# Decoder layer on one core: stores of keys issued by ScalarE, last pass in other parts, other ranks and buffers

## The chip, the core and the metric

The kernel runs on one core of a Trainium2 chip. Such a core has a tensor engine for matmuls (PE, with its weight loads shown as PEld), a vector engine (DVE), a scalar engine (ACT), GpSimd (POOL) and a sync engine (SP). Each takes its instructions strictly in the order of its own program; semaphores order them against each other. Transfers between DRAM and the on-chip memory (SBUF) are issued by an engine's queue and carried out by sixteen DMA engines. Matmuls write to PSUM, a small memory of eight banks, from which DVE or ACT copies.

The metric is the device time of one execution in microseconds; a kernel is run several times and the median is given. A profiled execution leaves a trace with every instruction, its start, its duration and what it waited for.

## The reference, cut to what matters

One inference step of a decoder layer: 512 new prompt tokens and 8 sample tokens of running sequences, model width 1024, float32. One projection of the input feeds two mixers, a gated linear attention (4 heads) and a dilated window attention (8 heads of 64); each result is multiplied by a SiLU gate, both go through one output projection, and a residual with LayerNorm closes the layer. The new keys and values are outputs too.

```python
SPLITS = (H_A * DK_A, H_A * DK_A, D_A, GATE_RANK, D_A, D_B, D_B, D_B, D_B)   # qa ka va za ga qb kb vb gb
...
for window, dil in DILATED_GROUPS:              # (128,1), (512,4), (2048,16)
    dist = jnp.arange(window // dil + 1) * dil
    idx = q_idx[:, None] - dist[None, :]        # row < 0 masked
    logits = einsum('bqhd,bqjhd->bhqj', q, k[idx]) * scale + rel_bias[t5_bucket(dist)]
    m = max(logits); p = exp(logits - m); s = sum(p)
    outs.append(einsum('bhqj,bqjhd->bqhd', p, v[idx]) / s)
...                                             # merged, weighted by their denominators
x = LayerNorm(alpha * x + concat(o_a * silu(g_a), o_b * silu(g_b)) @ w_out)
outputs: y_prompt, y_sample, state_gla_prompt, state_gla_sample, k_win_prompt, v_win_prompt, k_win_sample_new, ...
```

## The kernel before

**Arithmetic.** A float32 product is made of three matmuls in a faster format: a value is split into a high and a low part (`hi`, `lo`), and hi*hi, lo*hi and hi*lo are added in PSUM. ACT makes the high part of a weight, DVE the low part. PE runs one long list of such products, stage after stage (`ORDER`: qa, qb, kb, vb, gb and so on, the letters for query, key, value and gate of mixer a or b and a number for the column tile); this is the generator `dense`. Between the dense products stand the small matmuls of the mixers.

**Who sets the order.** No engine's order is written by hand. A planner in the kernel (`Plan`) takes tasks, which are generators that yield instructions, and at build time it takes in each step the instruction that could start first by its own table of costs (`Op.__init__`); among equals the lower rank goes first, the second argument of `add(task, rank)`. Instructions of PE that are not dense must be ready `SPARE` (800 ns) before their place. A transfer is costed with the time of its issue (`c`, another for SP than for the other issuer), a transfer time, and `LATE` when the DMA engines are thought to be busy. Buffers come from pools (`SLOTS`: `st` for strips, `t1` for small tiles, `w` for weights and so on), PSUM banks from three (`BANKS`: `d` for dense products, `s` for scores and weighted values, `t` for turns and other small ones). A task waits until its buffer is free. So a changed cost, rank or number of buffers moves instructions on all engines. Everything that is planned is recorded at line 377, and therefore tiles and not lines name things in the profile. In the listings below a number behind a name only tells one buffer from the next.

**The names that matter here.**
- `kw`: the new keys, turned into rows, in two tiles. `keys_store(i)` writes each to DRAM in eight stores of 64 KB, each as 512 runs of 128 bytes. `D` is SP's queue, `S` ACT and its queue, `V` DVE, `T` PE.
- `strip`: a strip of the table of position biases (`tabr`), 128 KB, one for two halves of a head's scores; DVE adds it to the scores (`pr<-ps_s,strip`) and takes their maximum, ACT makes the exponential (`pr`), PE turns the result (`ps_pt`), DVE or ACT copies it (`pt`), and PE multiplies with the values (`ps_pv`).
- `ps_turn`: values that are turned from columns to rows on PE, copied to `v`. `ps_sl`: scores of the sample tokens. Both take a `t` bank.
- `past`, `qbc`, `vv`, `pb`: the sample tokens' old keys, queries, old values and weights; POOL multiplies them, DVE reduces (`lt`, `o_pv`).
- `gb_s`: the sample tokens' gated result of mixer b. ACT and DVE split it (`mhb`, `mlb`); the first matmuls of the output projection (`ps_yf`) read both parts. `ps_oat`: the turned result of mixer a.
- `last_norm`: the last 128 rows of the output. DVE scales and shifts them in three parts, each stored as soon as it is ready. Four small operations on one column (`half`, `root`, in the profile `tail`) stand ahead.

## Time and profile before

| | us |
|---|---|
| median of three runs (276.99, 277.11, 278.33) | 277.11 |
| profiled execution | 277.73 |
| its span, from the first to the last instruction | 275.3 |
| PE busy | 266.1 |
| DVE busy | 214.0 |
| ACT busy | 157.5 |
| POOL busy | 54.3 |

The tensor engine's granted clock is 0.994 of full speed over the span. In the rows that follow, a time is followed by a duration; `out<-in` names what an instruction writes and reads; in square brackets stands the idle time of the engine just before, and what ended it. `SPq` and `ACTq` are the issues of transfers on SP and ACT; how long one takes is not how long the transfer takes. The table of stretches gives the busy time of each engine in a window of the span.

### The profile page before, as it was taken

How to read it: one execution, taken by the hardware profiler on the slowest of the kernel's cores; microseconds unless marked ns; L12 is line 12 of the kernel's file. 1: busy time of each engine (PE TensorE's matmuls, PEld its weight loads, DVE VectorE, ACT ScalarE, POOL GpSimd, SP SyncE). 2: the span in 40 equal slices, each digit the busy share in tenths (PEclk: the TensorE clock that was granted, in tenths of full speed). 3: DMA queues.
4: the chain of work that ended last, by engine and by line, in shares of the span. 5: the costliest groups of instructions: out<-in, count | busy, mean ns of one | idle time of the engine just before them, and what ended most of it. 6: DMA issues, size and time to landing. Idle time of an engine off the chain costs nothing.

```text
span 275.3 us, 7455 instructions
## 1 busy us (share of the span) xinstructions
PE 266.1 (97%) x2881; PEld 250.8 (91%) x2881; DVE 214.0 (78%) x582; ACT 157.5 (57%) x474; POOL 54.3 (20%) x71
## 2 busy tenths in 40 slices
PE   8999999999999999998999999999999999999990
PEld 5999999999999999987989989999999999998890
DVE  4835999998999587877696973737979999239984
ACT  4817966465637574957686824535668886224401
POOL 3000000000355080804000544745431000000000
PEclk9999999999999999999999999999999999999997
DMA  7977784436967798775497959896895660980432
GB/s 210 348 184 185 213 254 132 124 101 173 294 193 161 179 312 218 254 118 140 116 258 192 228 173 225 230 271 172 248 260 147 194 208 12 299 226 0 186 123 76
DMA packets 61527, 52.58 MB, mean 191 GB/s; under 512 B 13645, under 2 KB 53715, under 8 KB 61493
## 3 DMA queue, kind: packets, MB, share of 16 engines
q1 hardware_dynamic: 61061, 51.79, 67.6%
q8 instruction: 22, 0.36, 0.5%
q10 hardware_dynamic: 432, 0.33, 0.4%
q14 instruction: 12, 0.10, 0.1%
HBM read 46.02 MB, written 6.42 MB: 190 GB/s over the span
## 4 chain that ended last, share of the span: by engine, by line
PE 75%; DMA 9%; DVE 6%; SPq 4%; ACT 2%; issue 1%; POOL 1%; DVEq 0%; ACTq 0%
PE ps_ga L377 9%; PE ps_yf L377 9%; PE ps_qb L377 8%; PE ps_y L377 7%; PE ps_gb L377 6%; DMA strip<-tabr 6%; PE ps_qa L377 4%; PE ps_ka L377 4%; PE ps_va_f L377 4%; PE ps_va L377 4%; SPq L377 4%; PE ps_vb L377 3%; DMA qbc<-qsd 2%; PE ps_vb_f L377 2%; PE ps_pv L377 2%; ACT pr L377 2%
## 5 line engine op out<-in xcount | busy, mean ns | idle before, releaser
L377 POOL TENSOR_TENSOR past<-past,qbc 128x256 f32<-128x256 f32 x32 | 24.6, 803 | 101.1 <-DMA qbc<-qsd 92.4
L377 POOL TENSOR_TENSOR vv<-vv,pb 128x256 f32<-128x256 f32 x32 | 27.3, 887 | 51.9 <-DVE far L377 25.0
L377 ACT ACTIVATE pr<-pr,ms 128x128 f32<-128x128 f32 (+3 forms) x48 | 22.7, 489 | 9.7 <-DVE ms L377 9.6
L377 DVE CUSTOM_DVE_ANT_0 pr<-ps_s,strip 128x128 f32<-128x128 f32 (+3 forms) x32 | 11.7, 408 | 7.9 <-PE ps_s L377 4.4
L377 ACT COPY pt<-ps_pt 128x256 f32<-128x256 f32 (+1 forms) x26 | 8.9, 358 | 9.2 <-PE ps_pt L377 9.2
L377 ACT ACTIVATE sg<-sg 128x264 f32<-128x264 f32 (+1 forms) x32 | 13.4, 420 | 0.5
L377 PE MATMUL ps_ka<-xx,hi_ka 128*128 128x264 f32 (+1 forms) x64 | 12.5, 291 | 0.0
L377 PE MATMUL ps_pt<-cf,pr 128*128 128x128 f32 x56 | 10.8, 276 | 1.2 <-DVE v L377 1.2
L377 DVE TENSOR_REDUCE lt<-past 128x8 f32<-128x512 f32 x16 | 10.7, 673 | 1.1 <-POOL past L377 1.0
L377 PEld LDWEIGHTS ps_ka<-xx,hi_ka 128*128 128x128 f32 x64 | 10.1, 195 | 0.3 <-ACT hi_ka L377 0.3
L377 ACT ACTIVATE d<-d 128x512 f32<-128x512 f32 x11 | 6.9, 646 | 5.6 <-DVE d L377 5.6
L377 DVE TENSOR_REDUCE o_pv<-vv 128x4 f32<-128x1024 f32 x8 | 9.7, 1213 | 0.0
L377 ACT COPY feat_y<-ps_yf 128x256 f32<-128x256 f32 x7 | 2.6, 373 | 11.2 <-PE ps_yf L377 11.2
L377 PE MATMUL ps_ka<-xx,lo_ka 128*128 128x264 f32 (+1 forms) x32 | 8.7, 283 | 0.0
L377 PEld LDWEIGHTS ps_pt<-cf,pr 128*128 128x128 f32 x56 | 6.8, 140 | 1.7 <-DVE v L377 1.4
L377 DVE SCALAR_TENSOR_TENSOR y<-y,ps_yt 128x256 f32<-128x256 f32 x8 | 3.0, 418 | 6.9 <-PE ps_yt L377 6.9
L377 DVE SCALAR_TENSOR_TENSOR s<-v,ka_s,s 128x128 f32<-128x128 f32 x16 | 5.1, 343 | 3.2 <-DMA v<-vad 2.1
L377 PE MATMUL ps_qa<-xx,hi_ka 128*128 128x264 f32 (+1 forms) x32 | 7.2, 304 | 0.0
L377 PE MATMUL ps_s<-kp,qh 64*128 64x256 f32 (+1 forms) x64 | 7.0, 304 | 0.1
L377 PE MATMUL ps_pv<-pt,v 128*64 128x128 f32 (+1 forms) x80 | 6.9, 318 | 0.0
L377 DVE TENSOR_TENSOR d<-b 128x1024 f32<-128x1024 f32 (+1 forms) x6 | 6.8, 1129 | 0.0
L377 PE MATMUL ps_gb<-xx,hi_gb__1903 128*128 128x264 f32 (+1 forms) x32 | 6.8, 295 | 0.0
(570 smaller groups left out, 1060.7 us busy)
## 6 DMA issues: line engine op xcount, KB each, us to landing
past<-in_ck_dram SPq DMA_DIRECT2D x8, 512.0 KB
vv<-in_cv_dram SPq DMA_DIRECT2D x8, 512.0 KB
pb<-psd_s SPq DMA_DIRECT2D x16, 256.0 KB
s<-in_state_dram SPq DMA_DIRECT2D x4, 512.0 KB
strip<-tabr SPq DMA_DIRECT2D x16, 128.0 KB
qbc<-qsd SPq DMA_DIRECT2D x8, 256.0 KB
y<-in_xp_dram SPq DMA_DIRECT2D x4, 512.0 KB
x_raw<-in_xT_dram SPq DMA_DIRECT2D x6, 260.0 KB
```

What stands on the lines that cost most here:

```text
L377: getattr(eng.eng, op.fn)(*op.args, **op.kw)
```

## The change

The sixteen stores of `keys_store` are issued by ACT in place of SP. The last pass of `last_norm` goes in parts of 256, 512 and 256 columns in place of 512, 256, 256, with stores by ACT, SP and ACT in place of SP, ACT and SP, and the small operation `half` stands ahead of the wide one. One strip buffer fewer, one small tile more; four banks for scores and one for turns in place of three and two. In the planner's costs a transfer of an engine other than SP now takes 450 ns to issue, and a late one is 600 ns later. `va0` comes ahead of three `gb` tiles in the dense order. Sixteen ranks are new.

```diff
-    t2=2, st=3,
+    t2=2, st=2,
...
-    t1=5, ob=3,
+    t1=6, ob=3,
...
-BANKS = dict(d=3, s=3, t=2)
+BANKS = dict(d=3, s=4, t=1)
...
-LATE = 1000.0
+LATE = 1600.0
...
-ORDER = "qa0 qb0 qb1 qb2 qb3 kb0 kb1 vb0 kb2 kb3 gb0 vb1 gb1 gb2 va0 gb3 va1 ga0 ga1 ga2 ga3".split()
+ORDER = "qa0 qb0 qb1 qb2 qb3 kb0 kb1 vb0 kb2 kb3 gb0 vb1 va0 gb1 gb2 gb3 va1 ga0 ga1 ga2 ga3".split()
...
-            c = 640 if eng.name == "SP" else 100
+            c = 640 if eng.name == "SP" else 450
...
-                yield D.dma_start(kw_p[:, c:c + 32].rearrange("(b i) j -> i b j", i=32), kw[a * 32:a * 32 + 32, m])
+                yield S.dma_start(kw_p[:, c:c + 32].rearrange("(b i) j -> i b j", i=32), kw[a * 32:a * 32 + 32, m])
...
-        yield V.scalar_tensor_tensor(y[:, x], ps, mean, B["gamma"][:, x], op0=ALU.subtract, op1=ALU.mult)
         yield S.activation(root, ss, AF.Ln, scale=1.0 / DM, bias=q)
         yield V.tensor_scalar(half, ss, -0.5 / DM, dev, op0=ALU.mult, op1=ALU.add)
+        yield V.scalar_tensor_tensor(y[:, x], ps, mean, B["gamma"][:, x], op0=ALU.subtract, op1=ALU.mult)
...
-        for i, c in enumerate((slice(2 * GW, DM), slice(GW, 2 * GW), x)):
+        for i, c in enumerate((slice(3 * GW, DM), slice(GW, 3 * GW), x)):
             yield V.scalar_tensor_tensor(y[:, c], y[:, c], half, B["beta"][:, c], op0=ALU.mult, op1=ALU.add)
-            yield (S if i == 1 else D).dma_start(y_p[t * P:t * P + P, c], y[:, c])
+            yield (D if i == 1 else S).dma_start(y_p[t * P:t * P + P, c], y[:, c])
...
-    add(mix_sample_b(), 12.3)
+    add(mix_sample_b(), 18.3)
```

The other new ranks, before and after: `weight_splits` 50.7, 47.7; `gate_decay` 19.3, 1.7; `seed_sum` 13.2, 12.2; `bias_table` 25.3, 31.3; `sample_values` 14.3, 22.3; `sample_v` of `vnt` 21.3, 13.2 and of `vat` 21.3, 1.7; `sample_past` 22.3, 3.3; `sample_state` 61, 60; `values_store` 17.7, 17.3; `mix_tiles` 12.7, 11.7.

**The stores of keys.** SP's queue before, where the first tile of keys is stored; ahead of the stores stand the loads of a strip and of the sample's queries and keys, behind them strips:

```order
L377 DMA strip_1330<-tabr 128x1x256
L377 DMA strip_1330<-tabr 128x1x64
L377 DMA qbc_1305<-qsd 128x512
L377 DMA past_1380<-in_ck_dram 128x1024
L377 DMA out_dram<-kw_1133 32x16x32 x5
L377 DMA raw_vb__1415<-in_w_in_dram 128x4x256
L377 DMA out_dram<-kw_1133 32x16x32 x3
L377 DMA strip_1467<-tabr 128x1x256
L377 DMA strip_1467<-tabr 128x1x64
L377 DMA strip_1502<-tabr 128x1x256
```

ACT now, at the same tile:

```order
L377 ACTIVATE kp_1233<-ps_kb_1_1290 128x256
L377 COPY pt_1285<-ps_pt_1334 128x256
L377 DMA out_dram<-kw_1137 32x16x32 x2
L377 COPY pt_1285<-ps_pt_1378 128x128
L377 DMA out_dram<-kw_1137 32x16x32
L377 COPY vnt<-ps_vb_f_1345 128x8
L377 COPY feat<-ps_vb_f_1345 128x256
L377 DMA out_dram<-kw_1137 32x16x32
L377 ACTIVATE kd<-kd 128x1024
L377 ACTIVATE pr_1319,ms_1363<-pr_1319,ms_1363 128x128
L377 ACTIVATE pr_1319,ms_1364<-pr_1319,ms_1364 128x256
L377 ACTIVATE el<-b 128x16
```

Five and three stores in a row on SP are now two, one, one, one and three on ACT, between copies out of PSUM and exponentials; SP keeps its other rows.

**The strip of head 7 and the t bank.** The strip that DVE reads for head 7's first half, on SP: before (strip_2102; strip_1906 is head 5's) and now (strip_2218; strip_2031 is head 5's):

```order
L377 DMA out_dram<-kw_1717 32x16x32
L377 DMA qbc_1947<-qsd 128x512
L377 DMA strip_2102<-tabr 128x1x256
L377 DMA strip_2118<-tabr 128x1x256
L377 DMA strip_2118<-tabr 128x1x64
L377 DMA raw_va__2163<-in_w_in_dram 128x4x256
L377 DMA strip_2195<-tabr 128x1x256
```

```order
L377 DMA strip_2010<-tabr 128x1x256
L377 DMA strip_2031<-tabr 128x1x256
L377 DMA cts_raw<-in_c_t_dram 66x258
L377 DMA raw_gb__2154<-in_w_in_dram 128x8x128
L377 DMA strip_2196<-tabr 128x1x256
L377 DMA strip_2218<-tabr 128x1x256
L377 DMA raw_va__2272<-in_w_in_dram 128x4x256
L377 DMA strip_2287<-tabr 128x1x256
```

DVE now, from the second read of strip_2031 to the reads of strip_2218 (ISA is the addition with its maximum):

```order
L377 ISA pr_2159,ms_2178<-ps_s_2161,strip_2031 128x256
L377 ISA ms_2178 128x1
L377 RECIPROCAL ms_2177<-ms_2177 128x1
L377 TENSOR_SCALAR pr_2159<-pr_2159,ms_2177 128x128
L377 COPY v_1978<-ps_vb_3_2148 128x256
L377 RECIPROCAL ms_2178<-ms_2178 128x1
L377 TENSOR_SCALAR pr_2159<-pr_2159,ms_2178 128x256
L377 COPY pt_2052<-ps_pt_2209 128x256
L377 TENSOR_TENSOR lo_gb__2227<-raw_gb__1714,hi_gb__2226 128x1024
L377 ISA pr_2246,ms_2264<-ps_s_2248,strip_2218 128x128
L377 ISA ms_2264 128x1
L377 ISA pr_2246,ms_2265<-ps_s_2248,strip_2218 128x256
```

ACT now, in the same place; pr_2246 is what DVE makes with strip_2218:

```order
L377 ACTIVATE pr_2159,ms_2178<-pr_2159,ms_2178 128x256
L377 CAST hi_gb__2226<-raw_gb__1714 128x1024
L377 CAST hi_gb__2269<-raw_gb__1892 128x1024
L377 ACTIVATE pr_2246,ms_2264<-pr_2246,ms_2264 128x128
L377 ACTIVATE pr_2246,ms_2265<-pr_2246,ms_2265 128x256
L377 COPY v_1978<-ps_turn 128x2x128
L377 ACTIVATE pr_2245,ms_2262<-pr_2245,ms_2262 128x128
```

PE now; ps_turn is the bank that the COPY above reads, and ps_sl is the next in a `t` bank:

```order
L377 MATMUL ps_turn<-cf,feat 128x128 x2
L377 MATMUL ps_pv_2268<-far_1795,vp_1574 64x256
L377 MATMUL ps_pv_2268<-far_1833,vp_1574 64x256
L377 MATMUL ps_pv_2268<-far_2053,vp_1574 64x256
L377 MATMUL ps_pv_2268<-far_2084,vp_1574 64x256
...
L377 MATMUL ps_pv_2268<-pt_1794,v_1344 64x256 x2
L377 MATMUL ps_pv_2268<-pt_2052,v_1344 64x256 x2
L377 MATMUL ps_pv_2268<-pt_1794,v_1344 64x128 x2
L377 MATMUL ps_pv_2268<-pt_2052,v_1344 64x128 x2
L377 MATMUL ps_sl<-cts,rb 66x258
L377 MATMUL ps_va_f_2224<-xx_300,hi_va__1931 128x264
```

With two strip buffers, strip_2218 is loaded when strip_2031 has been read; with three, strip_2102 was loaded when the strip of head 4 had been read. The copy of ps_turn, which was DVE's, is ACT's and stands behind two exponentials of pr_2246, and PE's ps_sl waits for the bank.

**The split of gb_s.** DVE before, from the sum that completes gb_s to its low part, mlb:

```order
L377 TENSOR_TENSOR vnt<-vnt,o_pv 128x32
L377 TENSOR_REDUCE wsum<-raw_wo__3372 128x2
L377 TENSOR_TENSOR gb_s<-gb_s,vnt 128x32
L377 TENSOR_TENSOR newton<-rmss 128x4
L377 TENSOR_SCALAR ssq<-ssq 128x4
L377 CAST hi_wo__3586<-wsum 128x2x2
L377 TENSOR_TENSOR newton<-newton,ssq 128x4
L377 TENSOR_SCALAR ssq<-rmss 128x4
L377 TENSOR_TENSOR lo_wo__3587<-wsum,hi_wo__3586 128x2x2
L377 TENSOR_TENSOR mlb_2020<-gb_s,mhb_2019 128x2x8
L377 SCALAR_TENSOR_TENSOR rmss<-newton,ssq 128x4
L377 TENSOR_SCALAR oa_3156<-ps_oa_3510,rmss 128x128
```

DVE now:

```order
L377 TENSOR_TENSOR vnt<-vnt,o_pv 128x32
L377 TENSOR_REDUCE wsum<-raw_wo__3335 128x2
L377 TENSOR_TENSOR ga_3070<-ps_ga_0_3610,sg 128x256
L377 TENSOR_TENSOR ga_s<-ps_ga_0_3610,sg 128x8
L377 TENSOR_TENSOR gb_s<-gb_s,vnt 128x32
L377 CAST hi_wo__3625<-wsum 128x2x2
L377 SCALAR_TENSOR_TENSOR ga_s<-o_as,gn,ga_s 128x8x4
L377 SCALAR_TENSOR_TENSOR ga_3070<-ps_oat,gn,ga_3070 128x2x128
L377 TENSOR_TENSOR mlb_1982<-gb_s,mhb_1981 128x2x8
L377 TENSOR_TENSOR mla_3680<-ga_s,mha_3679 128x4x8
L377 SCALAR_TENSOR_TENSOR ga_3070<-ps_oat,gn,ga_3070 128x2x64
L377 TENSOR_TENSOR mlb_2764<-gb_s,mhb_2763 128x2x8
```

A gate (ga from ps_ga) now stands ahead of gb_s, and the first read of ps_oat ahead of mlb; the split stood in front of both.

22 lines of the change are left out of this document (11 added, 11 removed).

## The prediction

> **What bounds the kernel now.** I read the page first, then the table of stretches, the waits of the tensor engine, and the timeline at the one place where it waits. The page's busy line and its two hardware DMA queues (packets, MB, share of sixteen engines):
>
> ```profile
> PE 266.1 (97%) x2881; PEld 250.8 (91%) x2881; DVE 214.0 (78%) x582; ACT 157.5 (57%) x474; POOL 54.3 (20%) x71
> q1 hardware_dynamic: 61061, 51.79, 67.6%
> q10 hardware_dynamic: 432, 0.33, 0.4%
> ```
>
> PE is busy for 266.1 of 275.3 us, and the program of matmuls does not change, so what can be gained is a share of the 9.2 us in which PE stands. The waits of PE, and the stretches (stretch, its length, busy time of PE, PEld, DVE, ACT, POOL, granted clock, DMA share, GB/s):
>
> ```profile
> PE warm_ps L377 <- DVE warm L1844: 1.2, 1, 1.2
> PE ps_pt L377 <- DVE v L377: 1.2, 1, 1.2
> ```
> ```profile
> 125.00:150.00 25.00, 23.82 (x271) 21.76 (x266) 18.31 (x68) 17.02 (x54) 2.93 (x4) 1.00 0.64 176
> ...
> 250.00:275.00 25.00, 18.70 (x107) 16.01 (x106) 20.31 (x54) 6.74 (x27) 0.00 (x0) 0.94 0.29 106
> ```
> ```profile
> 75.00:95.00 20.00, 19.87 (x175) 19.30 (x174) 16.93 (x38) 12.15 (x34) 8.43 (x10) 1.00 0.70 174
> ```
>
> One wait stands at the start, which the change leaves; one lies in 125 to 150 us. Of the rest, 6.3 us are the tail after the last matmul, in the stretch from 250. This is a kernel bound by PE with one repairable hole. The hole in the timelines, PE and then DVE (start, duration, instruction, idle time before and its releaser):
>
> ```profile
> 127.58 0.28 PE L377 MATMUL ps_vb<-hi_vb__1584,xx 128*128 128x256 f32 x1
> 129.04 0.44 PE L377 MATMUL ps_pt<-cf,pr 128*128 128x128 f32 x2 [1.18 <-DVE v L377]
> ```
> ```profile
> 126.82 0.29 DVE L377 CUSTOM_DVE_ANT_0 pr<-ps_s,strip 128x128 f32<-128x128 f32 x1 [1.29 <-DMA strip<-tabr]
> 128.58 0.41 DVE L377 COPY v<-ps_turn 128x256 f32<-128x256 f32 x1
> ```
>
> DVE stood 1.29 us for a strip of the bias table; the copy of ps_turn stood behind that in DVE's order, and PE needed the bank that this copy frees. The strip was late behind the stores of keys: SP issued them in these pieces (with the strips just ahead), and the tile's row gives the least, median and greatest time of one; the last row is a store that ACT issued:
>
> ```profile
> 70.58 5.40 SPq L377 DMA_DIRECT2D strip<-tabr  x4
> ...
> 78.62 6.92 SPq L377 DMA_DIRECT2D out_dram<-kw  x5
> ...
> 86.14 2.47 SPq L377 DMA_DIRECT2D out_dram<-kw  x3
> ...
> 114.72 4.99 SPq L377 DMA_DIRECT2D out_dram<-kw  x6
> ```
> ```profile
> L377 SPq DMA_DIRECT2D out_dram<-kw x16: 315/530/1936, 78.6 to 120.2; - x16
> ```
> ```profile
> 271.79 0.36 ACTq L377 DMA_DIRECT2D out_dram<-y  x1
> ```
>
> **The change, part by part.** The sum is made against the profiled execution, 277.73 us (275.3 of span and 2.4 around it); that stands 0.6 above the runs' median of 277.11, which I take off at the end. 0.5% is 1.4 us, about what a measurement of this kernel can tell from no change.
>
> *The old stall, -1.2.* In the new order no PE instruction waits at that place on a DVE copy behind this strip's read: the dense stage of vb is over before the read. I count the 1.18 us as gone (between 0 and -1.3).
>
> *Two strips in place of three, +1.0.* Each strip load now waits for the read of the strip two before. The tight one is strip_2218. SP issues it after DVE's second read of strip_2031; ACT's copy of ps_turn stands behind the two exponentials of the scores that DVE reads with strip_2218; and ps_sl needs the bank of that ps_turn, since only one t bank is left. So a strip's flight again ends in a wait of PE. Its length is a race between two times from the last ps_s matmul of heads 4 and 5. The rows for it, from the chain, from DVE and from PE:
>
> ```profile
> 65.31 6.56 DMA strip<-tabr
> ...
> 121.19 5.49 DMA strip<-tabr
> ...
> 127.15 0.99 ACT pr L377 x4
> ...
> 129.63 1.42 PE ps_vb L377 x12
> ```
> ```profile
> 118.98 0.67 DVE L377 TENSOR_REDUCE lt<-past 128x8 f32<-128x512 f32 x1
> ...
> 119.94 0.24 DVE L377 CUSTOM_DVE_ANT_0 pr<-ps_s,strip 128x128 f32<-128x128 f32 x1
> ...
> 121.09 0.39 DVE L377 CUSTOM_DVE_ANT_0 pr<-ps_s,strip 128x256 f32<-128x256 f32 x1
> ...
> 122.97 0.36 DVE L377 TENSOR_SCALAR pr<-pr,ms 128x256 f32<-128x256 f32 x1
> ```
> ```profile
> 120.99 0.44 PE L377 MATMUL ps_s<-kp,qh 64*128 64x128 f32 x4
> ...
> 122.19 1.52 PE L377 MATMUL ps_pv<-far,vp 128*64 128x256 f32 x16
> ...
> 125.38 0.44 PE L377 MATMUL ps_turn<-cf,feat 128*128 128x128 f32 x2
> 125.65 0.27 PE L377 MATMUL ps_pt<-cf,pr 128*128 128x128 f32 x1
> ```
>
> The strip's side: the matmul's own 0.28; four reads of strips, which ran from 119.94 to 121.48, 1.5, with a reduction of lt (0.67), a scaling (0.36) and a copy (0.41) now among them: 3.0; flight 5.49; 0.14 until DVE starts (126.68 to 126.82); two reads to the end of the second, 0.6; its exponential, half of the four in 0.99, 0.5; the copy, 0.4. Sum 10.4; the nine instructions that DVE has between those reads are hidden in the flight. PE's side, up to ps_sl: 38 dense matmuls at 0.12 (twelve in 1.42), 4.5; six turns at 0.14 (two from 125.38 to 125.65), 0.8; twelve scores, 0.9 of the 1.2 from 120.99 to 122.19, which hold three dense ones too; the weighted values, 125.38 - 122.19 = 3.2. Sum 9.4. PE waits for 1.0. With a flight of 6.56 it is 2.1; with one under 4.5 it is 0. I take 5.49, the row of the same strip before, and keep 0 to 2.1.
>
> *ps_yf, +0.3.* The sample's gated attention output is now split at the last moment. Its rows before:
>
> ```profile
> 213.53 1.22 DVE L377 TENSOR_REDUCE o_pv<-vv 128x4 f32<-128x1024 f32 x1
> ...
> 217.31 0.17 DVE L377 TENSOR_TENSOR mlb<-gb_s,mhb 128x16 fp32r<-128x16 f32 x1
> ...
> 219.25 1.91 DVE L377 SCALAR_TENSOR_TENSOR ga<-ps_oat,gn,ga 128x256 f32<-128x256 f32 x6
> ```
> ```profile
> 217.92 1.03 PE L377 MATMUL ps_oat<-cf,oa 128*128 128x128 f32 x8
> ...
> 219.74 0.28 PE L377 MATMUL ps_yf<-mlb,hi_wo__3233 128*128 128x264 f32 x1
> ```
>
> Before, mlb was there at 217.48 for a matmul at 219.74, 2.3 us early. Now a read of ps_oat stands ahead of it on DVE. From the last ps_oat matmul DVE needs 0.28 of its own and 0.14 as above until it starts, 0.32 for the read (1.91 for six) and 0.17 for mlb: 0.9. PE needs 0.12 + six ps_ga and two ps_yf at 0.12: 1.1. That is 0.2 early if DVE is on time. If DVE is late by one o_pv reduction, which now stands shortly ahead, PE waits 1.0. I take 0.3, since the row of mlb shows DVE well in time, and keep 0 to 1.0.
>
> *Sixteen stores on ACT, +0.2.* SP spent at least 14.4 us in the three pieces quoted. On ACT an issue is engine time, so it delays copies out of PSUM. At 0.36 each the first eight cost 2.9 us beside ACT's 12.15 us in the 20 us from 75 to 95, where 7.85 are free: hidden by that idle time, except where a copy stands directly behind two or three stores (0.7 to 1.1 late). If it stays hidden the cost is 0; at SP's price for these eight, (6.92 + 2.47) / 8 = 1.17, they need 9.4 of 7.85 free, 1.5 late, and the second eight the same or less: 0 to 3. I take 0.2, nearer ACT's own row.
>
> [...]
>
> *SP without them, 0.* SP's rows come earlier by up to these 14 us, but strips are now held by the two buffers and weights by theirs. POOL gets its q rows sooner; nothing in PE's waits hangs on POOL.
>
> *The tail, -0.1.* The chain, and DMA in half microseconds:
>
> ```profile
> 269.82 0.13 DVE tail L377
> ...
> 270.61 0.75 DVE y L377
> ```
> ```profile
> 272.00:272.50 0.50, 0.00 (x0) 0.00 (x0) 0.15 (x1) 0.00 (x0) 0.00 (x0) 0.50 0.57 213
> ...
> 273.50:274.00 0.50, 0.00 (x0) 0.00 (x0) 0.00 (x0) 0.00 (x0) 0.00 (x0) 0.50 0.40 133
> ```
>
> The 0.13 us of the small operation leaves the chain. The first store can go 0.35 earlier, at half of the 0.75 pass; but the half-megabyte keeps the DMA engines full from 272.2 to 273.7, and its middle part, now the 512 columns, is ready only 0.13 earlier than the second part was. I take -0.1 (0 to -0.5).
>
> Sum: -1.2 + 1.0 + 0.3 + 0.2 - 0.1 = +0.2. 277.7 + 0.2 = 277.9, or 277.3 on the median's scale. The other ranks and buffers (ORDER, LATE, values, far) reorder work that PE did not wait for, by the rows above; I cost them at nothing, and what covers them is that no row of PE's waits names their results; where that cover is thinner than I think, rival 2 has it.
>
> **Rivals.** (1) *Slower: ACT is blocked while it issues.* If a store takes ACT what it took SP, the ACT copies behind it come late, and with a single t bank PE waits at once. It decides where an issue is dearer than 7.85 / 8 = 0.98 us. For it: the 1.17 above and the 1.936 maximum. Against: 0.36 on ACT. Price 1.5 for the first eight and up to 1.5 for the second, in place of the 0.2: 278.6 to 280.1, say 279.4. (2) *Slower: the flights are longer or several copies out of the one t bank meet.* The strip at 6.56 and ps_yf at its upper end add 1.8, and any further single-bank wait of a 0.4 us copy adds to it: 279.2. For it: POOL, DVE and SP already run in step with DMA. (3) *Faster: the new tight places hold.* With the stores gone from SP, flights fall under 4.5 us; -1.2 - 0.1 and nothing else gives 275.8, and with the upper ends of stall and tail, 275.3. For it: the strips before were queued with 128-byte stores. Against: a flight of 6.56 at 65 us, ahead of all stores.
>
> **How the numbers follow.** Forecast 0.43, ending 276.0 to 278.5. Rival 1 0.19, rival 2 0.17, rival 3 0.21. Rival 3 lies about the 0.5% line (275.7), so I put faster at 0.20, with a little of it for gains beyond; slower takes rivals 1 and 2, 0.36; same 0.44. The range goes from rival 3's best, 275.3, to rival 1's upper end, 280.1, and 0.2 over it for the copies of rival 2.
>
> **What would show it.** Right: no wait of ps_pt on v at about 128; a new wait of ps_sl on ACT's v of about 1 us at 130 to 140, with DVE waiting over 2 us for a strip; kw issues on ACT of about 0.4; a store of 128x512 that ends the tail. Wrong: kw issues above 1 us on ACT, or waits of PE on copies by ACT at 80 to 95 (rival 1); no wait of ps_sl (rival 3); waits of PE at other places, which I do not see.

## The result, and the profile after

| | before | after |
|---|---|---|
| median of six runs each on one chip (us) | 277.68 (276.99 to 278.64) | 280.63 (279.64 to 282.45) |
| profiled execution: span | 275.3 | 279.0 |
| of it: PE busy | 266.1 | 267.4 |
| PE idle up to the end of its last matmul | 2.6 | 4.1 |
| from there to the end of the span | 6.6 | 7.6 |
| DVE busy | 214.0 | 224.0 |

The changed kernel is slower: its time is 1.011 times that of the kernel before, 95% interval 1.0072 to 1.0147. The 3.7 us of span are 1.3 of PE's busy time, 1.5 of PE's idle time and 0.9 of tail. The forecast was 277.3 with a range up to 280.3.

The page of the changed kernel: the busy line, and the two queues of data (packets, MB, share of sixteen engines). ACT's queue q10 has the stores of keys now; DVE has 10 us more.

```profile
PE 267.4 (96%) x2881; PEld 251.7 (90%) x2881; DVE 224.0 (80%) x596; ACT 154.1 (55%) x460; POOL 54.5 (20%) x71
q1 hardware_dynamic: 52469, 50.61, 62.1%
q10 hardware_dynamic: 9024, 1.51, 2.9%
```

PE's waits (in all, times, longest), and the stretches (as in the table before: PE, PEld, DVE, ACT, POOL):

```profile
PE ps_kb L377 <- ACT qk L377: 1.7, 1, 1.7
PE warm_ps L377 <- DVE warm L1844: 1.2, 1, 1.2
PE ps_yf L377 <- ACT mhb L377: 1.1, 1, 1.1
```
```profile
50.00:75.00 25.00, 24.04 (x553) 22.54 (x552) 24.48 (x54) 14.88 (x41) 1.05 (x2) 1.00 0.50 144
75.00:100.00 25.00, 24.19 (x206) 23.92 (x207) 21.54 (x47) 13.66 (x40) 14.62 (x17) 1.00 0.80 227
...
125.00:150.00 25.00, 25.00 (x232) 23.47 (x231) 16.47 (x57) 13.63 (x38) 0.00 (x0) 1.00 0.59 170
...
200.00:225.00 25.00, 23.85 (x269) 22.69 (x270) 23.98 (x73) 18.26 (x67) 6.07 (x8) 1.00 0.71 211
```

The old hole in 125 to 150 is gone. Two new ones stand at 74 us (`ps_kb`) and at 220 us (`ps_yf`), at 1.75 and 1.12 us. The wait on a strip that the forecast expected at `ps_sl` is not there. Its rows, from DVE, SP, ACT and PE:

```profile
128.05 0.29 DVE L377 CUSTOM_DVE_ANT_0 pr<-ps_s,strip 128x128 f32<-128x128 f32 x1 [0.30 <-PE ps_s L377]
...
134.65 0.29 DVE L377 CUSTOM_DVE_ANT_0 pr<-ps_s,strip 128x128 f32<-128x128 f32 x1 [1.06 <-DMA strip<-tabr]
```
```profile
129.31 1.73 SPq L377 DMA_DIRECT2D strip<-tabr  x2
130.52 0.53 SPq L377 DMA_DIRECT2D strip<-tabr  x1
```
```profile
135.90 0.35 ACT L377 COPY v<-ps_turn 128x256 f32<-128x256 f32 x1
```
```profile
137.62 0.34 PE L377 MATMUL ps_sl<-cts,rb 66*66 66x258 f32 x1
```

The first of SP's two rows merges two loads, at 129.31 and 130.52; the second row is the later one alone. That is the strip that DVE waits for (strip_2218, by its semaphore): it landed at 134.52. DVE did wait 1.06 us for it, but ACT's copy of `ps_turn` ended at 136.25, 1.4 us before PE's `ps_sl`.

The hole at 74 us looks like a wait on ACT and isn't one. PE's rows, and the transfers from 73.5 to 74.6 us (q8 brings instructions, no data):

```profile
73.78 0.28 PE L377 MATMUL ps_kb<-xx,lo_kb__738 128*128 128x264 f32 x1
75.81 0.39 PE L377 MATMUL ps_kb<-xx,hi_kb__737 128*128 128x256 f32 x1 [1.75 <-ACT qk L377]
```
```profile
q1 hardware_dynamic: 238, 0.36, 90.5%
q8 instruction: 1, 0.02, 5.8%
```

In the trace the matmul of 75.81 waits on one semaphore, which ACT's instructions raise. ACT's `qk`, which the view names because it came last, ended at 75.39 here, but in four other traces of this order it ended after PE had gone on (in `same_again` at 74.70, PE went on at 74.31), so PE did not wait for it. What did land just before is one packet of 16 KB of instructions, from 73.53 to 74.56, 1.25 us before PE went on. q8 has 22 such packets in the span. Whether PE stood for this one is what the experiments put to the test.

The hole at 220 us is a wait on data. DVE's rows there:

```profile
218.18 1.21 DVE L377 TENSOR_REDUCE o_pv<-vv 128x4 f32<-128x1024 f32 x1
219.30 0.68 DVE L377 TENSOR_TENSOR lo_wo__3626<-raw_wo__3335,hi_wo__3625 128x512 fp32r<-128x512 f32 x1
219.90 0.19 DVE L377 TENSOR_TENSOR vnt<-vnt,o_pv 128x32 f32<-128x32 f32 x1
220.00 0.68 DVE L377 TENSOR_REDUCE wsum<-raw_wo__3335 128x2 f32<-128x512 f32 x1
220.60 0.42 DVE L377 TENSOR_TENSOR ga<-ps_ga,sg 128x256 f32<-128x256 f32 x1
220.93 0.16 DVE L377 TENSOR_TENSOR ga_s<-ps_ga,sg 128x8 f32<-128x8 f32 x1
221.00 0.19 DVE L377 TENSOR_TENSOR gb_s<-gb_s,vnt 128x32 f32<-128x32 f32 x1
```

DVE has no gap there; `gb_s`, which ACT splits into `mhb` for PE, stands behind a weight's low part, two `wsum` columns and a gate that PE did not need yet. But a low part and `wsum` stood there in the kernel before as well. Its row of `gb_s`, and POOL's last products `vv` in the changed kernel, which `o_pv` sums:

```profile
216.03 0.18 DVE L377 TENSOR_TENSOR gb_s<-gb_s,vnt 128x32 f32<-128x32 f32 x1
```
```profile
210.61 3.35 POOL L377 TENSOR_TENSOR vv<-vv,pb 128x256 f32<-128x256 f32 x4 [7.89 <-DMA pb<-psd_s]
```

From the start of `o_pv` to that of `gb_s` it took 2.50 us before (from 213.53) and takes 2.82 now. What moved is `o_pv` itself, by 4.65 us, while PE comes to its first `ps_yf` only 0.86 us later (219.50 before, 220.36 now without the wait). POOL's products ended at 213.96, 207.71 before, so DVE took them up 4.2 us after they were ready (5.8 before).

In the tail a block of instructions lands too. Transfers from 276 us to the end:

```profile
q10 hardware_dynamic: 129, 0.12, 11.2%
q14 instruction: 1, 0.01, 0.6%
```

This block of 8 KB lands 5.38 us after the last matmul, and SP's closing waits start 1.06 us behind it, at 6.44. The first of them is for the last store of `y`, whose semaphore gets sixteen signals in these traces: fifteen came by 5.38 us after the last matmul, the sixteenth at 6.42. In `before_new_tail`, with no block of instructions there, all sixteen had come by 5.35.

### The profile page after: what moved, and what is told of

Same layout as the page of the kernel before. It is cut to its first block, busy times and chain, and to the rows that moved or that the text cites. A ratio compares the mean times of both kernels' runs of the same rounds, so it can differ in the third digit from the quotient of the medians.

```text
span 279.0 us, 7440 instructions
## 1 busy us (share of the span) xinstructions
PE 267.4 (96%) x2881; PEld 251.7 (90%) x2881; DVE 224.0 (80%) x596; ACT 154.1 (55%) x460; POOL 54.5 (20%) x71
## 3 DMA queue, kind: packets, MB, share of 16 engines
HBM read 46.02 MB, written 6.42 MB: 188 GB/s over the span
## 4 chain that ended last, share of the span: by engine, by line
PE 83%; DVE 11%; ACT 3%; issue 1%; DVEq 0%
PE ps_yf L377 9%; PE ps_qb L377 8%; PE ps_gb L377 8%; PE ps_y L377 8%; PE ps_kb L377 7%; PE ps_qa L377 4%; PE ps_ka L377 4%; PE ps_va_f L377 4%; PE ps_vb_f L377 4%; PE ps_vb L377 4%; PE ps_va L377 4%; PE ps_s L377 3%; PE ps_pv L377 2%; PE ps_l L377 2%; PE ps_pt L377 2%; DVE o_pv L377 2%
## 5 line engine op out<-in xcount | busy, mean ns | idle before, releaser
L377 POOL TENSOR_TENSOR past<-past,qbc 128x256 f32<-128x256 f32 x32 | 26.9, 872 | 94.4 <-DMA qbc<-qsd 74.6
L377 POOL TENSOR_TENSOR vv<-vv,pb 128x256 f32<-128x256 f32 x32 | 25.3, 821 | 64.6 <-DMA pb<-psd_s 61.5
L377 ACT ACTIVATE pr<-pr,ms 128x320 f32<-128x320 f32 (+3 forms) x44 | 21.4, 501 | 12.2 <-DVE ms L377 11.9
L377 PE MATMUL ps_pt<-cf,pr 128*128 128x128 f32 x56 | 11.4, 274 | 0.0
L377 PEld LDWEIGHTS ps_ka<-xx,hi_ka 128*128 128x128 f32 x64 | 10.4, 201 | 0.0
L377 DVE TENSOR_SCALAR pr<-pr,ms 128x128 f32<-128x128 f32 (+3 forms) x20 | 9.2, 470 | 0.1
L377 PE MATMUL ps_kb<-xx,hi_kb__737 128*128 128x264 f32 (+1 forms) x32 | 6.2, 292 | 1.7 <-ACT qk L377 1.7
L377 DVE TENSOR_TENSOR far<-tp,same 128x128 f32<-128x128 f32 (+1 forms) x16 | 7.5, 491 | 0.0
```

The costliest lines, as they stand in the source:

```text
L377: getattr(eng.eng, op.fn)(*op.args, **op.kw)
```

## The experiments

The theories at the start: F, PE's instructions at 74 us come late; D, a copy on ACT is late there; T, the tail costs; A, the stores cost by what the plan's price of 450 moves from ACT to DVE (14 instructions, most of DVE's 10 us more). G and T2 came later and are told in the expectations. Ratios are to the kernel before in the same series. The PE idle times below are gaps between matmuls in the traces.

**The kernel as it is, twice more, and the tail alone.** `before_new_tail` is the kernel before with the new `last_norm`; `after_old_tail` the changed kernel with the old one; `same_again` has no edit.

```diff
-        for i, c in enumerate((slice(2 * GW, DM), slice(GW, 2 * GW), x)):
+        for i, c in enumerate((slice(3 * GW, DM), slice(GW, 3 * GW), x)):
...
-            yield (S if i == 1 else D).dma_start(y_p[t * P:t * P + P, c], y[:, c])
+            yield (D if i == 1 else S).dma_start(y_p[t * P:t * P + P, c], y[:, c])
```

> The changed kernel once more, unaltered, for a second profile. Theory F (late instructions): the hole of PE at 73.8 to 75.8 us is not a wait for data, since all that its matmul waits for was there by 68.8 us; PE stands because its next block of instructions arrives late behind data transfers. Then the hole comes again near 74 us, between 1 and 2.5 us long, with the instruction block of 16 KB landing inside it, and its length follows the landing. Theory D (a late copy of ps_kb on ACT): the hole ends 0.05 us after the copy of qk in this profile too. The hole at ps_yf comes again with 1.0 to 1.5 us under both. Time 280.6, 1.011 of before.

> The kernel before with the new last pass alone (parts of 256, 512, 256 columns, stores by ACT, SP, ACT, the small operation ahead of the wide one); all else stands in the same order. Theory T (the new tail costs): from the end of the last matmul to the end of the span it takes 7.4 to 7.6 us in place of 6.6, and the time is 0.7 to 0.9 us longer, 1.003. Rival, the prediction's term: 6.5 us and 0.1 less, 1.000.

> The changed kernel with the old last pass; all ahead of it stands in the same order. Theory T: 6.6 us after the last matmul, 0.7 to 0.9 us faster than the changed kernel, 1.008 of before. Rival: no difference, 1.011. For the hole near 74 us it is a third profile: under F it comes again with another length, under D it ends with the copy of qk.

Measured: 280.76 (1.013, 1.0069 to 1.019), 277.47 (1.0011, 0.9978 to 1.0045), 280.61 (1.0127, 1.0054 to 1.0199). The loss repeats. Both new holes were there in the first and the third, 0.94 and 1.50 at `ps_kb`, 1.5 and 1.5 at `ps_yf`. The new tail alone takes 6.49 us after the last matmul in place of 6.64, as forecast; in the changed order it takes 7.54 to 7.56, the old one 6.94. The time with the old tail is no shorter (1.0127 and 1.013), as the rival of theory T said.

**The stores, through the plan.** Three kernels change one part and let the planner order everything anew: the changed kernel with the stores on SP; the kernel before with the stores on ACT and the price of 450; the changed kernel with the price at 100.

```diff
-                yield S.dma_start(kw_p[:, c:c + 32]...
+                yield D.dma_start(kw_p[:, c:c + 32]...
```
```diff
-            c = 640 if eng.name == "SP" else 450
+            c = 640 if eng.name == "SP" else 100
```

(the second kernel has both lines the other way round, in the kernel before)

> The changed kernel with the sixteen stores of keys back on SP and all else new; the planner then orders all engines anew. Theory A (the stores on ACT are what costs, by ACT's time and the copies that go to DVE instead): ACT's copies go back to ACT, DVE is busy for 216 us in place of 224, ps_yf is not late, the time is 1.000 to 1.004 of before. Rival (ranks, banks and buffers cost it): no better than the changed kernel, 1.009 or more.

> The kernel before with one part of the change: the sixteen stores of keys from ACT, and ACT's price of 450 in the plan; ranks, buffers, banks and tail are those of before. Theory A (the stores cost nothing themselves, but the price moves copies from ACT to DVE): issues of about 0.34 us on ACT, no wait of ps_pt on v at 128 us (-1.2), DVE's busy time 3 to 8 us above 214, and a new wait of PE on DVE or ACT of up to 1.5 somewhere; time 276.3 to 278.3. Rival (ACT stands while it issues): issues above 0.9, waits of PE on ACT's copies between 80 and 120 us, 278.6 to 280.1.

> The changed kernel with the plan's price of an issue on ACT put back from 450 to 100; the stores stay on ACT. The plan then gives ACT again some fourteen copies and scalings that it had moved to DVE. Up to 76 us nothing moves. Theory A (the loaded DVE is late at the end of the sample, and that makes PE wait at ps_yf): DVE's busy time falls from 224 to 214 to 219, PE's wait at ps_yf falls from 1.1 to 1.5 us to under 0.5, while the wait at ps_kb (0.9 to 1.7) stays; time 278.8 to 279.8. Rival (the ranks, not DVE's load, make that wait): the wait at ps_yf stays at 1.0 or more and the time at 280 to 281.

Measured: 323.6 (1.157, 1.1459 to 1.1678), 297.16 (1.0687, 1.0611 to 1.0764) and 289.13 (1.0399, 1.0318 to 1.0479). The first is 43 us above the changed kernel, where its rival had said only 1.009 or more; the second and third are 17 and 8 us above anything expected. In the first PE waits 34.4 us at `ps_yf`, in the second 9.6, in the third 3.5 and 3.4 at `ps_oat`: the sample's work ends far too late. The second also waits 5.7 at `ps_turn` for a copy by ACT, of which more below. The ranks fit one set of prices only; of a single part such a kernel says little. All later ones therefore keep the planned order and change what is issued.

**The stores alone, with the order kept.** The plan counts the stores where it did; only the queue that issues them differs.

```diff
-        getattr(eng.eng, op.fn)(*op.args, **op.kw)
+        unit_eng = self.engines["ACT"].eng if op.fn == "dma_start" and op.args[1].tensor.name.startswith("kw") else eng.eng
+        getattr(unit_eng, op.fn)(*op.args, **op.kw)
```

(in the second, in the changed kernel, `"SP"` for `"ACT"`)

> The kernel before, with the sixteen stores of keys issued by ACT in place of SP and nothing else changed: the plan still counts them on SP, so all other instructions keep their order on every engine. By the terms of the forecast: no wait of ps_pt on v at 128 us (-1.2), issues of 0.34 us on ACT that hide (+0.2, at most +0.6), SP's rows up to 14 us earlier: 276.3 to 277.1 where the kernel before gives 277.4. Rival (ACT's copies come late behind the stores, 0.7 to 1.1 each): new waits of PE on ACT between 78 and 125 us of 1 to 3 us in all, 277.5 to 280.

> The changed kernel with the sixteen stores issued by SP again and nothing else changed: the plan still counts them on ACT, so all other instructions keep their order. If the stores' queue matters by itself (the strips, of which there are two buffers now, come late behind stores that cost SP about 1 us each): new waits of PE between 85 and 130 us of 1 to 4 us, 281.5 to 284. If it does not: 280 to 281, and all that the change lost comes from order and count.

Measured: 285.57 (1.0295, 1.0234 to 1.0356) and 279.39 (1.0066, 1.0026 to 1.0106). In the first the issues are as cheap as forecast, and yet ACT stood. Its rows, and PE's:

```profile
79.00 5.12 ACTq L377 DMA_DIRECT2D out_dram<-kw  x4
84.17 0.17 ACT L377 COPY vnt<-ps_vb_f 128x8 f32<-128x8 f32 x1 [4.80 <-DMA out_dram<-kw]
...
86.27 3.73 ACTq L377 DMA_DIRECT2D out_dram<-kw  x2
90.10 1.06 ACT L377 ACTIVATE kd<-kd 128x1024 f32<-128x1024 f32 x1 [5.49 <-DMA strip<-tabr]
```
```profile
92.77 0.69 PE L377 MATMUL ps_turn<-cf,feat 128*128 128x128 f32 x2 [4.67 <-ACT feat L377]
```

The four issues of 0.32 to 0.50 us take 5.12 because the fourth starts at 83.81, 2.7 us after the third is done. In the trace a store waits on the same semaphore that it will signal, so it stands until the transfer that used it before has landed: the fifth, at 86.27, waits for the third, issued at 80.76. With the copies behind it, PE waits 4.67 and 0.94 us. ACT stands in the changed kernel too. Its rows there:

```profile
90.16 2.85 ACTq L377 DMA_DIRECT2D out_dram<-kw  x2
93.05 1.05 ACT L377 CAST hi_gb__1568<-raw_gb__1081 128x1024 fp32r<-128x1024 f32 x1 [2.57 <-PE ps_vb L377]
```

The second of these stores starts at 92.68, 2.0 us after the first is done (2.6 in `same_again`); the transfer that used its semaphore before, a strip that SP issued at 88.42, landed at 92.66. But behind it stands the cast of a weight and no copy that PE waits for, and PE has no idle time from 82 to 120 us. So a store on ACT cost PE nothing where nothing that PE needs soon stood behind it. The second kernel shows what the stores' place is worth there: PE's last matmul ends at 271.18, with 271.47 in the changed kernel, and PE's idle time is 3.75 for 4.06: nothing that stands out from run to run. The time is 1.2 lower, and the tail in its trace is 6.50 in place of 7.56 (below); the intervals of the two ratios overlap (1.0026 to 1.0106 and 1.0072 to 1.0147), so that the time fell for this is not shown.

**The stop at 74 us.** If PE stood for that packet, it stood where one block of its instructions ends and the next had not landed. Two kernels shift that place: the warm-up matmuls of 512 columns are issued in halves, all seven (14 instructions more) or one (2 more; its edit halves the first of them only).

```diff
-        getattr(eng.eng, op.fn)(*op.args, **op.kw)
+        halves = [slice(0, 256), slice(256, 512)] if op.fn == "matmul" and op.args[0].tensor.name.startswith("warm_ps") else []
+        for args in [(op.args[0][:, h], op.args[1], op.args[2][:, h]) for h in halves] or [op.args]:
+            getattr(eng.eng, op.fn)(*args, **op.kw)
```

> Each of the seven warm-up matmuls of 512 columns is issued as two of 256: the same columns in all, but 14 more instructions on PE ahead of everything else; no other instruction moves on any engine. Theory F (PE's instructions come late): PE stands where a block of instructions ends, so the stop moves with the count, 14 records earlier in the program, that is seven matmuls ahead of the end of the first part (264 columns) of ps_kb, and PE stands between two matmuls of 264 columns of one sum, where no data can be waited for. The stop is as long or longer (1.0 to 2.8 us), since PE gets there about 0.8 us sooner. Theory D (the first matmul of the second part waits for a copy on ACT or a bank): the stop stays at the first matmul of 256 columns, 0.9 to 1.9 us. Time under both 280 to 282.

> One of the seven warm-up matmuls is issued as two of 256 columns: 2 more instructions on PE ahead of everything else, nothing else moves. Theory F (PE stands where a block of its instructions ends): the stop at about 73.8 us comes one matmul sooner, between two matmuls of 264 columns of one sum of ps_kb, and ends 1.2 to 1.4 us after the block has landed; or, if the block lands before 72.3 us, there is none. Theory D: the stop is at the first matmul of 256 columns, as in the changed kernel.

Measured: 280.26 (1.0076, 1.0036 to 1.0115) and 281.89 (1.0158, 1.0076 to 1.0241). PE's rows and wait in the second:

```profile
73.76 0.41 PE L377 MATMUL ps_kb<-xx,hi_kb__738 128*128 128x264 f32 x2
75.99 0.28 PE L377 MATMUL ps_kb<-xx,lo_kb__739 128*128 128x264 f32 x1 [1.82 <-issue]
```
```profile
PE ps_kb L377 <- issue: 1.8, 1, 1.8
```

Two instructions more, and the stop comes exactly one matmul sooner, between two matmuls of one sum, and the view names no releaser but the issue: this matmul waits on no semaphore at all. D is out. With 14 more there is no stop at all: PE runs through from 69.99, and the block landed at 71.13. That it would be as long or longer was wrong.

The third kernel holds back two loads of 512 KB, to see whether the block stands behind them:

```diff
+        held += [op] if name.startswith(("raw0_vb1", "past2")) else []
+        for o in [op] * (op not in held) + held * name.startswith("strip30"):
+            getattr(o.eng.eng, o.fn)(*o.args, **o.kw)
```

> Two loads of 512 KB that SP issues at 70.3 (raw_vb) and 71.3 us (past) are issued after the two strips of 73 us instead; what they bring is first read at 94 us and after 78 us. Nothing else moves. Theory F (PE's block of instructions stands behind these loads in the DMA engines): with 1 MB less ahead of it the block that PE needs at about 73.8 us lands by 72.6 or sooner in place of 74.6, and PE's wait at ps_kb is under 0.7 us or gone, in place of 1.7; time 1.0 to 1.7 below that of the changed kernel, 279.0 to 279.8. Theory D (a copy on ACT is late): the wait stays at 0.9 to 1.9 us and the time at 280 to 281.

Measured: 280.33 (1.0091, 1.0056 to 1.0126); the block lands at 73.60, the stop is 1.46. So it is not these loads. Over the runs with the changed order and PE's program as it was, or two longer, the block's landing and PE's going on (from the single transfers and matmuls in the traces):

```
run                          block lands   PE goes on   after   stop
after_kw_on_sp_same_order       72.71        74.09      1.38    0.37
after_early_gate                72.83        74.28      1.45    0.72
same_again                      73.08        74.31      1.23    0.94
after_held_loads                73.60        74.96      1.36    1.46
after_old_tail                  73.76        75.12      1.36    1.50
after_dve_two_more              74.44        75.81      1.37    1.76
after                           74.56        75.81      1.25    1.75
after_block_shift_2             74.56        75.99      1.43    1.82
after_scalings_on_act           71.72        (no stop)
```

PE goes on 1.23 to 1.45 us after its block has landed, whenever that is. In the three runs with all warm-ups halved the block landed at 71.0 to 71.2, and there was no stop. In all eight traces with the stop it stands behind the same 1985 records of PE (matmuls, weight loads and semaphore waits), although in `after_block_shift_2` that is another matmul. A second stop of the kind, of 0.38 to 0.57 us, stands at 54 to 56 us in four traces (`after_dve_two_more`, `after_kw_on_sp`, `after_price_100`, `before_kw_on_act_same_order`), behind record 1217, which is 768 records earlier; PE went on 1.36 to 1.57 us after the landing of a block. The last of the four has the order of before, so such a stop is not the changed order's alone. In the traces of `before` and `before_new_tail` the block landed at 71.29 and 70.78, and PE reached the end of the one ahead at 72.9 and 73.1, so there was time. What makes it land later in the changed order is open.

**The wait at 220 us.** Three DVE instructions are issued behind `mlb`.

```diff
+        held += [op] * (self.issued in (3026, 3035, 3049))
+        for o in [op] * (op not in held) + held * last:
+            getattr(o.eng.eng, o.fn)(*o.args, **o.kw)
```

> Three instructions of DVE that stand among those that end the sample's gated output (the second half of lo_wo at 219.30, the sums wsum at 220.00, 0.68 us each, and a small copy of wsum) are issued directly after mlb, some 1.5 us later; nothing else moves. Theory A (PE waits at ps_yf because DVE has these ahead of gb_s): gb_s ends 1.4 sooner, PE's wait at ps_yf falls from 1.1 to 1.5 us to under 0.3. If PE keeps that, the time is 279.2 to 279.8, 0.9 to 1.4 under the changed kernel; if what follows is bound elsewhere (Theory G, given back), the wait goes, others of the same sum take its place and the time is 280.2 to 281. If the wait stays above 0.8, neither holds.

Measured: 280.59 (1.0105, 1.0018 to 1.0192). `gb_s` started 1.76 us after `o_pv` (217.46 to 219.22) in place of 2.82, 1.06 sooner for the 1.4 expected; the wait on `mhb` fell to 0.45, but the second `mlb` now stood behind the three and PE waited 0.84 for it. So the place of these three makes part of the wait, and what was gained ahead of them was lost behind them.

**The tail.** Two small memsets of DVE, doubled at the very start:

```diff
+        for _ in range(1 + (eng.name == "DVE" and op.fn == "memset" and op.args[0].tensor.name.startswith(("sums_s", "pn_r")))):
             getattr(eng.eng, op.fn)(*op.args, **op.kw)
```

> Two small memsets of DVE at the very start are issued twice: DVE has two instructions more, nothing else moves. Theory T2 (the late block of instructions in the tail is DVE's, and whether it falls into the tail hangs on DVE's count; a run with 707 DVE instructions had it at 2.1 us after the last matmul, those with 706 at 5.1): with 708 the block comes at or before 2.1 us, the tail from the last matmul to the end of the span falls from 7.55 to 6.5, and the time by 1.0, to 279.4 to 279.9. Rival (the tail was shorter in that run because the stores were on SP): the tail stays at 7.4 to 7.6 and the time at 280.4 to 280.8.

The block now starts 2.1 us after the last matmul in place of 5.1 (transfers from 275 to 276.5 us; PE ended at 273.60 in this run):

```profile
q1 hardware_dynamic: 27, 0.02, 3.1%
q14 instruction: 1, 0.01, 1.8%
```

and the tail falls from 7.56 to 6.50, as T2 has it. Over the traces with the planned order kept the tail goes with the number of DVE's instructions, semaphore waits among them: 706 of them gave 7.54 to 7.58 (five runs), 705 gave 6.80 and 6.94, 698 to 700 and 707 to 708 gave 6.49 to 6.64. The time did not follow: 280.47 (1.0115, 1.0075 to 1.0155), where T2 had 279.4 to 279.9. The traced execution is the slowest of its six, with PE's end 2.1 later than in `after` and 5.2 of idle time, so it does not say where the others lost the microsecond. So the tail's microsecond is shown in the traces, not in this kernel's time.

**All three at once**, the seven halved warm-ups, the doubled memsets, and the three DVE instructions behind both `mlb`:

```diff
-        held, last = ..., op.args[0].tensor.name.startswith("mlb0") and "gb_s" in op.args[1].tensor.name
+        held, last = ..., op.args[0].tensor.name.startswith("mlb1") and "gb_s" in op.args[1].tensor.name
```

> The changed kernel with three repairs that change no result: the seven warm-up matmuls in halves (PE's blocks end 14 instructions earlier), the three DVE instructions lo_wo, wsum and its copy issued behind both mlb of the sample, and the two memsets twice. If the pieces add and PE keeps them (1.3 at ps_kb, 1.2 at ps_yf, 1.05 in the tail): 277.0 to 277.8, about the time of the kernel before. If the time is bound by DVE as well and PE gives back what it gains (Theory G): the waits at ps_kb and ps_yf go, others of 1 to 2 us take their place, and only the tail is kept: 279 to 280.

Measured: 279.24 (1.0072, 1.0047 to 1.0097), within the 279 to 280 of theory G. The changed kernel had 280.63 (1.011); the intervals of the two ratios overlap. Tail 6.50; no stop at 74 us; but PE's last matmul ended at 271.46, as in the changed kernel. Its waits now:

```profile
PE ps_s L377 <- DVE kp L377: 1.1, 1, 1.1
PE ps_yf L377 <- ACT mhb L377: 0.4, 1, 0.4
PE ps_oat L377 <- DVE ga L377: 0.4, 1, 0.4
```

The 1.1 at `ps_s` starts at 77 us, right behind the stop that was taken away: DVE's `kp` is not ready. So the stop hid a wait on DVE of 1.1 (0.46 to 1.11 in the four traces of this order without the stop), and what one repair gains the next wait takes.

**Is DVE's load that next wait?** The last eight scalings of `oa` that the plan gave to DVE are issued on ACT, in the changed kernel and together with the three repairs.

```diff
+        o = next(h[0] for h in self.alts if h[0].eng.name == "ACT") if self.issued in (2833, 2836, 2900, 2904, 2908, 2950, 2955, 2959) else op
+        getattr(o.eng.eng, o.fn)(*o.args, **o.kw)
```

> In the changed kernel the last eight scalings of the attention output (oa) that the plan gave to DVE, at 205 to 215 us, are issued on ACT at the same places; all else keeps its order. Theory G (DVE's load between 200 and 225 us is a wall that every gain before it runs into; the price of 450 helped to build it): DVE's busy time in that stretch falls from 24.0 to 21.5 to 22.5, PE's idle time there from 1.1 to 2.1 us to under 0.6, and the time, with DVE's count at 698 and so the short tail (-1.05), to 278.2 to 279.3. Rival (the wall is the sample's chain through POOL and its loads, not DVE): PE's idle time there stays above 1.0 and the time falls by the tail alone, to 279.4 to 279.8.

> The three repairs (PE's blocks end 14 instructions earlier, three DVE instructions behind the sample's gate, short tail) and the eight scalings on ACT in one. Theory G: with the wall taken down the gains before it are kept; PE's idle time is 2.6 to 3.2 us in all in place of 4.1 to 4.6, the time 277.2 to 278.4, within 0.5% of the kernel before. Rival: PE's idle time between 200 and 225 us stays above 1.0 and the time at 279 or more.

Measured: 280.86 (1.011, 1.0057 to 1.0162) and 280.09 (1.0078, 1.0048 to 1.0107). The stretch and PE's wait in the first:

```profile
200.00:225.00 25.00, 22.85 (x252) 21.55 (x251) 20.96 (x61) 19.47 (x72) 6.19 (x8) 0.95 0.66 186
```
```profile
PE ps_yf L377 <- ACT mhb L377: 1.5, 1, 1.5
215.98 0.42 DVE L377 TENSOR_TENSOR ga<-ps_ga,sg 128x256 f32<-128x256 f32 x1 [1.24 <-ACT sg L377]
```

DVE's busy time fell to 20.96, more than expected, and PE's wait stayed at 1.5, as the rival had it. DVE now stood itself, 1.04 and 1.24 us, for `sg`, which ACT makes from a bank that PE has just filled; `gb_s` stands behind these gates in DVE's order. So less load on DVE did not bring `gb_s` sooner (it started at 221.19 us, at 221.00 in `after`); `o_pv` and `gb_s` stand behind gates that hang on PE's own last matmuls. Theory G falls in this form. PE's idle time by stretch of the span:

```
                             0-10  60-82  82-120  120-135  200-225   sum   last matmul ends
before                       1.19   0.13    0       1.18      0      2.64     268.70
before_new_tail              1.19   0       0       1.30      0      2.48     268.76
after                        1.19   1.75    0       0        1.12    4.06     271.47
after_block_shift            1.19   0.45    0.60    0        2.10    4.35     271.26
after_early_gate             1.19   0.72    0.07    0        1.48    3.46     270.84
after_three_repairs          1.53   1.11    0.28    0        1.34    4.26     271.46
after_scalings_on_act        1.29   0.62    0.48    0        2.15    4.54     273.21
after_repairs_and_scalings   1.44   0.70    0.75    0        1.55    4.54     271.75
```

**The old stall without the change.** The kernel before, with the new tail, and with seven stores on SP moved behind the strip whose flight ended in the stall:

```diff
+        held += [op] * (op.fn == "dma_start" and op.args[1].tensor.name.startswith("kw1") and self.issued > 1590)
+        for o in [op] * (op not in held) + held * (op.fn == "dma_start" and op.args[0].tensor.name.startswith("strip70")):
+            getattr(o.eng.eng, o.fn)(*o.args, **o.kw)
```

> The kernel before with the new tail, and with seven stores of keys on SP moved behind one load of a strip (the one whose flight ended in the old stall at 127 us): SP can issue that strip from about 120.9, when its buffer is read, in place of 121.19, and no store flies with it. If the stores made that flight long (5.49 us): it is under 4.5, PE's wait of ps_pt on v falls from 1.2 to under 0.4, and the time is 276.0 to 276.8, under both kernels. If the flight is as long without them (6.56 us was seen at 65 us, ahead of all stores): the wait stays at 0.8 or more and the time at 277.0 to 277.8.

Measured: 276.73 (0.9974, 0.9946 to 1.0001). The strip's issue on SP, DVE's read of it, and PE's waits:

```profile
121.92 0.55 SPq L377 DMA_DIRECT2D strip<-tabr  x1
122.52 5.21 SPq L377 DMA_DIRECT2D out_dram<-kw  x7
```
```profile
126.34 0.29 DVE L377 CUSTOM_DVE_ANT_0 pr<-ps_s,strip 128x128 f32<-128x128 f32 x1 [0.17 <-DMA strip<-tabr]
```
```profile
PE warm_ps L377 <- DVE warm L1844: 1.2, 1, 1.2
PE ps_oa L377 <- ACT sg L377: 0.6, 1, 0.6
PE ps_s L377 <- DVE kp L377: 0.3, 1, 0.3
```

The flight, to the landing at 126.20, is 4.28 in place of 5.49, and the wait of `ps_pt` on `v` is gone: the stores issued directly ahead of the strip in the same queue made it. PE keeps part of it (0.9 of new waits). The kernel is well under the changed one (0.9974 and 1.011 of before); against the kernel before the interval just touches no change, and 0.15 of the gain is the new tail's.

## Why the prediction was wrong

It said +0.2 on the profiled execution; the span grew by 3.7. Term by term:

| term of the sum | forecast | measured in the trace after |
|---|---|---|
| the old stall | -1.2 | -1.2, gone as said |
| two strips in place of three | +1.0 (0 to 2.1) | 0; copy 1.4 early |
| `ps_yf` | +0.3 (0 to 1.0) | +1.1 (1.0 to 1.5 in the other traces of that order) |
| sixteen stores on ACT | +0.2 (0 to 3) | 0 on PE; issues of 0.338 in the median |
| SP, other ranks and buffers | 0 | +1.75 at `ps_kb`, +1.3 of PE's busy time, -0.2 of small holes |
| the tail | -0.1 (0 to -0.5) | +0.9 |

*The old stall* was right in place and size, and `before_stores_after_strip` shows its cause. That run also shows that it could be had without the rest of the change.

*Two strips* failed in the strip's side, which was worked out at 10.4 us and took 8.5 (from the start of the last `ps_s` matmul at 127.74 to the copy's end at 136.25). The step "four reads of strips ... 3.0" came near: SP issued strip_2218 at 130.52, directly behind the fourth read, 2.5 us after the matmul's end. The step that failed is "flight 5.49": it took 4.0, from 130.52 to 134.52 (3.95 to 4.74 in six other traces of this order). The 5.49 was the row of a strip with stores of keys directly ahead of it in SP's queue, and `before_stores_after_strip` shows 4.28 for the same strip without them; in the changed kernel none stand ahead. The prediction's own condition, "with one under 4.5 it is 0", is what came, as rival 3 had it for the flights. PE's side, worked out at 9.4, took 9.9.

*ps_yf* was the right place with the wrong part. The step looked at `mlb` and at DVE's last 0.9 us; PE waited for `mhb`, for which `gb_s` must be there. It took DVE to be "well in time" from a row of the old order, where `mhb` was ready 3.05 us early (216.45 for 219.50). In the new order `o_pv` starts 4.65 later, and the low part, `wsum` and the gate between it and `gb_s`, 1.6 us, were not counted either. That "If DVE is late by one o_pv reduction" gives about the right size, 1.0, is luck: `o_pv` is late by more than its own length.

*Sixteen stores*: the price of an issue was right (0.338 for 0.36), and rival 1, an issue dearer than 0.98, did not come. `before_kw_on_act_same_order` shows what the rival should have been: not the price of the issue, but a wait ahead of it until an earlier transfer has landed, 2.7 us in one case, with PE's copies behind. In the changed kernel that wait is there too, 2.0 us at 92.7, with nothing behind it that PE needed.

*The other ranks, costed at nothing*: this is the step that lost most, and with it the prediction. Its cover, "that no row of PE's waits names their results", holds for the order in which the rows were taken; with a new order PE meets other things. The stop at `ps_kb` is not even a result of an engine but a block of PE's own program, and the 1.3 of PE's busy time is spread over many tiles, none above 0.5 (traces of the changed order have 266.6 to 268.7, those of before's order with the stores on SP 266.1 to 267.0; the means are 267.3 of twelve and 266.4 of three, so part of the 1.3 is scatter). Rival 2 had only "any further single-bank wait" for this; its 279.2 fell 1.4 short. "Waits of PE at other places, which I do not see" was the sign of being wrong that came.

*The tail*: the change of the last pass did what was forecast where it was tried alone, 0.15. The 1.05 on top come from a block of DVE's instructions that the changed count moved into the last microseconds, where the last store's sixteenth signal came a microsecond late (6.42 us after the last matmul; all had come by 5.35 in `before_new_tail`).

What stays open: why PE's block lands later in the changed order, which of the new ranks puts `o_pv` and `gb_s` where they are, what the rest of PE's longer busy time is, and why PE's idle time returns at other places (3.5 to 5.4 in all traces of this order with the stores on ACT) when a named wait is removed.

## What to carry to other kernels

A row of the old order is no price in the new one where the change takes away what made it: the flight of 5.49 held the stores that were to go, and the early `mlb` an `o_pv` that was to move. A tuned plan's numbers belong together: one part undone through the planner cost 8 to 43 us and told little, so keep the order and move single instructions when a cause is to be isolated. A wait that the view puts down to an engine which ended after the waiting instruction had started in another run is not that wait; look for a block of instructions that lands just before (here 1.25 us before PE went on), and put two instructions more ahead of it to be sure (here the stop came one matmul sooner). Before removing a wait, ask what would be late directly behind it: here the stop at 74 us hid a DVE copy that was as late.

## What the runs showed of the hardware that was not expected

q8 brought instructions in 22 packets of 16 KB, and in eight traces PE stood for 0.37 to 1.82 us at one place of its program, until 1.23 to 1.45 us after one of these packets had landed; with two instructions more on PE the stop came one matmul sooner. In four traces PE stood 768 records earlier, for 0.38 to 0.57 us. At the other packets PE's waits show no such stop: `after` has one at 22 packets, `before` none. At the stop of `after` the DMA engines were 90.5% busy with data; that this made the block late is not shown. The block that moves with DVE's count is 8 KB on q14. With 706 DVE instructions it started 5.1 us after the last matmul, beside the last store, and the tail was 7.54 to 7.58 us; with 707 and 708 it started 2.1 us after, and the tail was 6.50. A store on ACT, 0.338 us to issue in the median of `after`, held ACT there for 2.0 us, for 2.6 in `same_again` and 2.7 in `before_kw_on_act_same_order`, while it waited until an earlier transfer that used its semaphore had landed, in the changed kernel one that SP had issued.
